# Half of the gate weights: the rounding remainder made by an adding transfer instead of a subtraction

## The chip, the cores and the metric

The kernel runs on one core of a Trainium2 chip. The core has an engine for matrix products (TensorE, in the profile PE, its weight loads PEld), three for elementwise work (VectorE or DVE, ScalarE or ACT, GpSimd or POOL), a queue that only issues transfers (SyncE or SP) and 16 DMA engines that carry out the transfers of all queues. Each engine works through its own instructions in a fixed order and waits on semaphores for the others. The metric is the device time of one execution in microseconds (us).

## What is computed

Two decoder layers over 512 tokens of width 2048: a Mamba-2 mixer in layer 0 and a stick-breaking attention in layer 1, each followed by a gated embedding. The change touches only the last, which stands in the reference once for each layer:

```python
for i in range(DEPTH):                       # DEPTH = 2
    u = rms_norm(h, norm_w[i])
    mix = ssd_branch(u, ...) if i % 2 == 0 else sb_branch(u, ...)
    h = h + mix
    gate = jax.nn.sigmoid((rms_norm(h, ple_norm_w[i]) @ ple_gate_w[i]))    # 2048 x 2048 weights
    h = h + (p[i] @ ple_proj_w[i]) * gate                                  # 256 x 2048 weights
```

## The kernel before

**Products.** Activations lie transposed, 128 channels on the partitions and 512 tokens along the free dimension, so a 2048-wide tensor is 16 tiles. A float32 product is made of three products in TensorE's faster, rounded 32-bit format (F32R). Weights and activations are split into a rounded part (`wh`, `ah`) and the remainder (`wl`, `al`), and `mm3` issues wh·ah, wh·al and wl·ah into one PSUM tile.

**Blocks.** Weights come in blocks of 8 tiles of 128 by 128 (512 KB, 128 partitions by 1024 numbers). `block` (L130 to L138) loads one from HBM over SP into `raw` (two buffers), ACT copies it into `wh` with rounding (three buffers), DVE subtracts, `wl = raw - wh` (three buffers), and TensorE uses it for 24 products of 512 columns.

**Gate stages.** `ple` (L513 on) runs once per layer. It splits the 16 tiles of `h` (`norm_acts`, L505), starts the norm's factor `rbc` from `ssq`, the sum of squares that POOL adds up (L503), and then makes 16 units of 128 output channels, j = 0 to 15, called u0 to u15 below. A unit is six products for p W in the PSUM tile `px_p` and a call of `unit` with two blocks, b0 and b1, 48 products in the PSUM tile `mm`. Behind them DVE multiplies by `rbc` (L532), ACT takes the sigmoid (L533), DVE multiplies by `px_p` (L534) and adds to `h` (L535). In layer 0 the square of the new `h` is then added to `ssq` (ACT L502, POOL L503), in layer 1 the tile of `h` goes out (L539). Every fourth unit also needs a block of `w_ple`, which keeps one of the three `wh` and `wl` buffers for four units; the other two pass between b0 and b1.

**Order.** TensorE's order is that of the program, by the class `Flow`. On the other engines a scheduler sets it when the kernel is built. `block` runs at high priority, so its steps stand as early as its buffers allow. The order is fixed on each engine, and an instruction that waits holds up all behind it.

Of the kernel before, what the change touches and what calls it, by code (L numbers as in the profile page):

```python
# [9 lines left out]
F32 = mybir.dt.float32  # L10
F32R = mybir.dt.float32r
AF = mybir.ActivationFunctionType
ALU = mybir.AluOpType
# [17 lines left out]
class Flow:  # L31
    """The tensor engine's instructions in the order in which they are traced.

    Side work is a generator that yields how many microseconds of products
    are to pass before it goes on, so that its operands are there by then."""

# [46 lines left out]
def trunk(  # L83
# [23 lines left out]

# [1 line left out]
    cst = cpool.tile([P, 4, P], F32, name="cst")  # L109
# [18 lines left out]

# [1 line left out]
    def block(src, offset=4000):  # L130
        with tc.high_priority(offset=offset):
            raw = wp.tile([P, 8, P], F32, tag="raw", name="raw", bufs=2)
            nc.sync.dma_start(raw, src)
            wh = wp.tile([P, 8, P], F32R, tag="wh", name="wh")
            S.copy(wh, raw)  # L135
            wl = wp.tile([P, 8, P], F32R, tag="wl", name="wl")
            V.tensor_tensor(wl, raw, wh.bitcast(F32), op=ALU.subtract)  # L137
        return wh, wl  # L138
# [15 lines left out]
    def staged(pool, tags, src, k0, k1):  # L154
        """Operands from tiles k0 to k1 of what was set down in DRAM."""
        acts = []
        for k in range(k0, k1):
            tag, bufs = tags[k % len(tags)]
            raw = pool.tile([P, T], F32, tag=tag, name="stg", bufs=bufs)
            nc.sync.dma_start(raw, src[k * P : (k + 1) * P, :])  # L160
            acts.append(act_tiles(k % KT))
            split(*acts[-1], raw)
        return acts
# [9 lines left out]

    def unit(src, acts):
        """One tile of 128 output channels: src is [128, nk, 128] in DRAM."""
        ps = mmp.tile([P, T], F32, tag="mm", name="mm")
        n = len(acts)
        for b in range(n // 8):
            wh, wl = block(src[:, 8 * b : 8 * b + 8, :])
            for k in range(8):  # L180
                kk = 8 * b + k
                mm3(ps, wh[:, k, :], wl[:, k, :], acts[kk][0], acts[kk][1], kk == 0, kk == n - 1)
                fl.poll()
        return ps

    def rsqrt(dst, ps, eps):
        """dst = (ps + eps) ** -0.5, with one Newton step behind the tables."""
        a = rp.tile([P, T], F32, tag="rsa", name="rsa")
        S.activation(a, ps, AF.Ln, bias=eps)
        S.activation(dst, a, AF.Exp, scale=-0.5)  # L190
        V.tensor_tensor(a, dst, dst, op=ALU.mult)
        V.scalar_tensor_tensor(a, ps, eps, a, op0=ALU.add, op1=ALU.mult)
        V.tensor_scalar(a, a, -0.5, 1.5, op0=ALU.mult, op1=ALU.add)
        V.tensor_tensor(dst, dst, a, op=ALU.mult)

    def act_set(name):
        """Loads a set of tables next after the ACT instructions so far."""
        with tc.high_priority(offset=100000):
            tc.keep_in_program_order(S.preload_act_table_set(name))

    def silu(dst, half, tmp):
        """x sigmoid(x) from x / 2: (tanh(x / 2) + 1) x / 2."""
        S.activation(tmp, half, AF.Tanh)  # L203
        S.activation(tmp, tmp, AF.Identity, bias=1.0)  # L204
        G.tensor_tensor(dst, half, tmp, op=ALU.mult)  # L205

    def row_scale(rbc, ssq, delay):
        """The norm's factor of each token, on every partition."""
        yield delay
        ps = px("px_n")  # L210
        fl.mm(ps, onesd, ssq)
        rsqrt(rbc, ps, eps6[:, 0:1])
# [5 lines left out]

    # ======== layer 0: SSD mixer ========
    with ExitStack() as st:  # L220
# [5 lines left out]
        acts = []  # L226
# [27 lines left out]

        # dt for the 64 heads and the first tile of B, side by side
        psd = mmp.tile([P, T], F32, tag="mm", name="psd")
# [17 lines left out]
        def dt_job():  # L274
            """dt = softplus(raw + bias), by token; the sums of a dt within chunks."""

# [7 lines left out]
            S.activation(e, e, AF.Exp, scale=-1.0)  # L284
            # log1p(e) = 2 atanh(e / (2 + e))
            V.tensor_scalar(z, e, 2.0, None, op0=ALU.add)
# [34 lines left out]

        # the convolution gives half of what silu takes
        V.tensor_scalar(vec[:, 128:368], vec[:, 128:368], 0.5, None, op0=ALU.mult)
# [18 lines left out]
        def scan(g, BT, CT, xc, zs):  # L342
            """The group's chunk scan, gate and norm."""
            hs = slice(g * HG, (g + 1) * HG)
            yield 11.0
            xdt, xw = [], []
            for c in range(NC):
# [18 lines left out]
                if c == 1:  # L366
                    # scores by source token, zero where the source comes later
                    pss = px("px_sc")
                    for c_ in range(NC):
                        cs = slice(c_ * P, (c_ + 1) * P)  # L370
                        fl.mm(pss[:, cs], BT[:, cs], CT[:, cs])
                    scT = sp.tile([P, NC, P], F32, tag="scT", name="scT")
                    V.tensor_tensor(
                        scT, pss.rearrange("p (c l) -> p c l", l=P), tri.unsqueeze(1).broadcast_to([P, NC, P]), op=ALU.mult
                    )
                    psb = px("px_bt")
                    for c_ in range(NC - 1):
                        fl.transpose(psb[:, c_ * P : (c_ + 1) * P], BT[:, c_ * P : (c_ + 1) * P], ident)
                    Bh = sp.tile([P, (NC - 1) * P], F32R, tag="Bh", name="Bh")
                    Bl = sp.tile([P, (NC - 1) * P], F32R, tag="Bl", name="Bl")  # L380
                    split(Bh, Bl, psb[:, : (NC - 1) * P])
                yield 4.0
                if c >= 1:
                    # states at the chunks' ends, [n, (h p)]
                    e = c - 1
# [96 lines left out]

        # the first units of the output projection, beside the last scan
        acts = staged(sp, [(f"xc{i}", 2) for i in range(4)], y_d, 0, KT)
# [7 lines left out]

    # ======== from here on the residual stays on chip ========
    lp = ctx.enter_context(tc.tile_pool(name="lp", bufs=1, reuse_waits="tile"))
# [18 lines left out]
    def ple(lq, layer, ssq):  # L513
        """h += (p W) sigmoid(norm(h) Wg), by tiles of 128 channels."""
        acts = norm_acts(plw[layer])
# [7 lines left out]
        for j in range(KT):  # L523
            if j % 4 == 0:
                vh, vl = block(w_ple[layer, j // 4])
            psp = px("px_p")
            for k in range(2):
                kk = 2 * (j % 4) + k
                mm3(psp, vh[:, kk, :], vl[:, kk, :], ph[:, k, :], pl[:, k, :], k == 0, k == 1)
            ps = unit(w_gate[layer, j], acts)  # L530
            gt = lq.tile([P, T], F32, tag="gt", name="gt", bufs=2)
            V.tensor_tensor(gt, ps, rbc, op=ALU.mult)  # L532
            S.activation(gt, gt, AF.Sigmoid)  # L533
            V.tensor_tensor(gt, psp, gt, op=ALU.mult)  # L534
            V.tensor_tensor(h[j], h[j], gt, op=ALU.add)  # L535
            if layer == 0:
                add_sq(lq, nssq, j)
            else:
                nc.sync.dma_start(out[j * P : (j + 1) * P, :], h[j])  # L539
# [17 lines left out]

    # ======== layer 1: stick-breaking attention ========
    with ExitStack() as st:
# [8 lines left out]
        def token_scale():  # L568
            """The factor of each token as one column to a chunk."""
            yield 20.0  # L570
# [7 lines left out]
        def values(m):  # L578
            """v of four heads by token, split."""
            pv = [mmp.tile([P, T], F32, tag="mm", name="pv") for _ in range(NC)]  # L580
# [42 lines left out]
        def attend(hd, done, vals):  # L623
# [9 lines left out]
            def scores(i):  # L633
# [5 lines left out]
                else:  # L639
                    mm3(pz, kh[:, ks], kl[:, ks], qh[:, qs], ql[:, qs])  # L640
                # log sigmoid(z) and -log sigmoid(-z)
                e = ap.tile([P, T], F32, tag="e", name="e", bufs=2)[:, :n]
# [12 lines left out]
                if i < NC - 1:  # L655
                    # with the same rows of the later blocks of sources
                    V.tensor_tensor(lm[:, P:], lm[:, P:], A[i + 1][2], op=ALU.add)
# [75 lines left out]

        # the first half of some output units, beside the last head
        half = staged(ap, [("stg", 3)], o_d, 0, 8)
# [19 lines left out]
def _units(w, cols):  # L755
    """[K, N] -> [units, 128 of K within a tile, K tiles, 128 columns]."""
    k = w.shape[0] // P
# [54 lines left out]
```

## Time and profile before

| | |
|---|---|
| two runs | 2759.84 and 2762.78 us, median 2761.31 us |
| span of the profiled execution | 2757.8 us |
| TensorE busy | 2732.7 us, 99% of the span |
| VectorE, ScalarE, GpSimd busy | 58%, 43%, 13% |
| HBM traffic | 108 GB/s on average |

The profiled execution has no time of its own beside its span, from the first to the last instruction. The span lies 3.5 us under the median of the runs, and what lies around it is not in the profile. Each gate stage takes some 200 us: the first from about 1373 to 1570 us, the second from about 2555 us to the end.

### The profile page before, as it was taken

Reading aid. Unit: us, or ns where it says so; the run is one execution under the profiler, and the core shown is the slowest. Engines: PE = TensorE matmul, PEld = TensorE weight load, DVE = VectorE, ACT = ScalarE, POOL = GpSimd, SP = SyncE. Lnnn points to the kernel's source line nnn. Section 1 sums busy time; section 2 is a strip of 40 time slices with the busy share of each in tenths; the row PEclk is TensorE's granted clock in tenths of the full one; section 3 lists DMA queues with packets and bytes.
Section 4 is the critical chain, followed back from the end, with each engine's and each line's share of the span. In section 5 each row is a group of like instructions: output and inputs, shape, how many; then the busy total and the mean of one; then the engine's idle time right before and its main releaser. Section 6 shows DMA issues by size and latency. Waiting matters only on the chain.

```text
span 2757.8 us, 32622 instructions
## 1 busy us (share of the span) xinstructions
PE 2732.7 (99%) x12684; PEld 2247.4 (81%) x12684; DVE 1597.3 (58%) x2226; ACT 1188.0 (43%) x1700; POOL 358.4 (13%) x363
## 2 busy tenths in 40 slices
PE   8999999999999999999999999999999999999999
PEld 6888888888888878888888888888888888888887
DVE  8676766676676774243443547647647647743533
ACT  5443444444353442232333436546646546533321
POOL 2222221212222120001101100000000000011000
PEclk9999999999999999999999999999999999999999
DMA  4342323233332446343323322322222222332332
GB/s 160 109 130 92 130 92 126 93 118 106 116 123 97 141 137 202 119 139 98 96 95 100 96 96 85 100 96 84 87 90 92 81 95 89 110 126 100 107 116 91
DMA packets 98348, 300.53 MB, mean 109 GB/s; under 512 B 10960, under 2 KB 11088, under 8 KB 98192
## 3 DMA queue, kind: packets, MB, share of 16 engines
q1 hardware_dynamic: 98192, 298.44, 33.2%
q8 instruction: 99, 1.62, 0.2%
q14 instruction: 57, 0.47, 0.1%
HBM read 280.18 MB, written 18.22 MB: 108 GB/s over the span
## 4 chain that ended last, share of the span: by engine, by line
PE 89%; DVE 5%; ACT 2%; POOL 2%; DMA 1%; issue 1%; SPq 0%; ACTq 0%; POOLq 0%; DVEq 0%
PE mm L54 74%; PE pv L54 6%; PE px_p L54 2%; DVE wl L137 1%; DVE M L410 1%; PE px_r L54 1%; PE px_z L54 1%; PE px_av L54 1%; POOL y L437 1%; PE px_st L54 1%; ACT wh L135 1%; PE px_y L54 1%; DMA stg<-y_d 1%; DVE cv L339 1%; PE px_qn L54 1%
## 5 line engine op out<-in xcount | busy, mean ns | idle before, releaser
L54 PE MATMUL mm<-ah,wh 128*128 128x512 f32 x3312 | 1300.1, 393 | 1.0 <-ACT ah L142 1.0
L54 PE MATMUL mm<-ah,wl 128*128 128x512 f32 x3312 | 1291.7, 390 | 0.0
L54 PE MATMUL mm<-al,wh 128*128 128x512 f32 x3312 | 1290.1, 390 | 1.5 <-DVE al L143 1.3
L137 DVE TENSOR_TENSOR wl<-raw,wh 128x1024 fp32r<-128x1024 f32 x457 | 569.9, 1247 | 492.3 <-ACT wh L135 491.2
L135 ACT CAST wh<-raw 128x1024 fp32r<-128x1024 f32 x457 | 478.7, 1048 | 856.7 <-PE mm L54 729.2
L54 PEld LDWEIGHTS mm<-ah,wl 128*128 128x128 f32 x3312 | 621.6, 188 | 131.9
L54 PEld LDWEIGHTS mm<-al,wh 128*128 128x128 f32 x3312 | 622.1, 188 | 130.9 <-DVE al L143 3.9
L54 PEld LDWEIGHTS mm<-ah,wh 128*128 128x128 f32 x3312 | 622.0, 188 | 126.3 <-ACT ah L142 1.2
L503 POOL TENSOR_TENSOR ssq<-ssq,sq 128x512 f32<-128x512 f32 x45 | 71.8, 1596 | 620.0 <-ACT sq L502 620.0
L410 DVE TENSOR_SCALAR M<-ab,act__370 128x128 f32<-128x128 f32 x256 | 104.8, 452 | 41.1 <-PE px_y L54 27.9
L339 DVE SCALAR_TENSOR_TENSOR cv<-xr,vec,cv 128x512 f32<-128x512 f32 x144 | 108.7, 755 | 7.0 <-ACT cv L337 4.4
L650 POOL TENSOR_SCALAR_AFFINE_SELECT lm<-lm 128x128 f32<-128x128 f32 x64 | 28.0, 438 | 615.3 <-DVE lm L649 609.6
L54 PE MATMUL pv<-wh,ah 128*128 128x512 f32 x256 | 101.0, 395 | 0.3 <-DVE gt L532 0.3
L54 PE MATMUL pv<-wl,ah 128*128 128x512 f32 x256 | 99.9, 390 | 0.0
L54 PE MATMUL pv<-wh,al 128*128 128x512 f32 x256 | 99.7, 389 | 0.0
L532 DVE TENSOR_TENSOR gt<-mm,rbc 128x512 f32<-128x512 f32 x32 | 22.1, 691 | 103.6 <-PE mm L54 103.6
L205 POOL TENSOR_TENSOR xc<-cv,sg 128x512 f32<-128x512 f32 x32 | 42.6, 1331 | 262.0 <-ACT sg L204 262.0
L203 ACT ACTIVATE sg<-cv 128x512 f32<-128x512 f32 x48 | 30.4, 633 | 104.6 <-DVE cv L339 104.3
L647 DVE SCALAR_TENSOR_TENSOR lb<-px_z,e 128x128 f32<-128x128 f32 (+1 forms) x64 | 31.4, 490 | 72.7 <-ACT e L645 72.2
L417 ACT ACTIVATE eA<-ab 64x384 f32<-64x384 f32 x64 | 33.6, 525 | 62.8 <-POOL y L437 60.3
L205 POOL TENSOR_TENSOR zs<-zs,sg 128x512 f32<-128x512 f32 x32 | 41.6, 1300 | 139.0 <-ACT sg L204 128.6
L337 ACT ACTIVATE cv<-xr,vec 128x512 f32<-128x512 f32 x48 | 39.0, 812 | 45.2 <-DVE xr L335 45.2
(219 smaller groups left out, 2557.9 us busy)
## 6 DMA issues: line engine op xcount, KB each, us to landing
raw<-in_w_in SPq DMA_DIRECT2D x160, 512.0 KB, 3.6
raw<-in_w_sb SPq DMA_DIRECT2D x96, 512.0 KB, 3.6
raw<-in_w_out SPq DMA_DIRECT2D x64, 512.0 KB, 3.9
raw<-in_w_gate SPq DMA_DIRECT2D x64, 512.0 KB, 3.5
ab<-ac_d SPq DMA_DIRECT2D x64, 256.0 KB, 3.2
raw<-in_w_v SPq DMA_DIRECT2D x32, 512.0 KB, 3.6
raw<-in_w_sbo SPq DMA_DIRECT2D x32, 512.0 KB, 3.5
y_d<-zs SPq DMA_DIRECT2D x32, 256.0 KB, 4.3
```

The costliest lines, as they stand in the source:

```text
L54: self._queue(self.tc.nc.tensor.matmul(out, lhsT, rhs, start=start, stop=stop), rows / 2370.0)
L135: S.copy(wh, raw)
L137: V.tensor_tensor(wl, raw, wh.bitcast(F32), op=ALU.subtract)
L203: S.activation(tmp, half, AF.Tanh)
L205: G.tensor_tensor(dst, half, tmp, op=ALU.mult)
L337: S.activation(cv, xr[:, 3 : T + 3], AF.Identity, bias=cb[:, u : u + 1], scale=cw[:, u, 3:4])
L339: V.scalar_tensor_tensor(cv, xr[:, tap : tap + T], cw[:, u, tap : tap + 1], cv, op0=ALU.mult, op1=ALU.add)
L410: V.tensor_scalar(M[:, c, :], ab[:, c * P : (c + 1) * P], act_[:, c, h : h + 1], act_[:, c, h : h + 1], op0=ALU.min, op1=ALU.subtract,)
L417: S.activation(eA[pp, :], ab[pp, P:], AF.Exp)
L503: G.tensor_tensor(ssq, ssq, sq, op=ALU.add)
L647: V.scalar_tensor_tensor(lb, pz, 0.0, e, op0=ALU.min, op1=ALU.subtract)
L650: G.affine_select(out=lm[:, :P], in_=lm[:, :P], compare_op=ALU.is_gt, fill=0.0, base=0, pattern=[[1, P]], channel_multiplier=-1,)
```

## The change

In the 16 units of each gate stage, b1 (`b % 2 == 1`) no longer gets its remainder from DVE. ACT writes the negated copy, `wl = -wh`, and a transfer from SBUF to SBUF on POOL's queue adds `raw` to it, `wl += raw`. b0, the blocks of `w_ple` and all other weights stay as they were. It concerns 32 of 457 blocks. Lines of the changed kernel lie seven further down from here on; comments and docstrings were taken out, which changes nothing.

```diff
-    def block(src, offset=4000):
+    def block(src, offset=4000, add=False):
         with tc.high_priority(offset=offset):
             raw = wp.tile([P, 8, P], F32, tag="raw", name="raw", bufs=2)
             nc.sync.dma_start(raw, src)
             wh = wp.tile([P, 8, P], F32R, tag="wh", name="wh")
             S.copy(wh, raw)
             wl = wp.tile([P, 8, P], F32R, tag="wl", name="wl")
-            V.tensor_tensor(wl, raw, wh.bitcast(F32), op=ALU.subtract)
+            if add:
+                S.mul(wl, wh.bitcast(F32), -1.0)
+                G.dma_start(wl, raw, accum_op=ALU.add)
+            else:
+                V.tensor_tensor(wl, raw, wh.bitcast(F32), op=ALU.subtract)
         return wh, wl
...
-    def unit(src, acts):
+    def unit(src, acts, add=False):
         ps = mmp.tile([P, T], F32, tag="mm", name="mm")
         n = len(acts)
         for b in range(n // 8):
-            wh, wl = block(src[:, 8 * b : 8 * b + 8, :])
+            wh, wl = block(src[:, 8 * b : 8 * b + 8, :], add=add and b % 2 == 1)
...
-            ps = unit(w_gate[layer, j], acts)
+            ps = unit(w_gate[layer, j], acts, add=True)
```

ACT in the second gate stage, units 0 to 2, before. The `gt` rows are the sigmoids of u0, u1 and u2; the two `wh` rows ahead of each are b0 and b1 of the next unit.

```order
L533 ACT_TABLE_LOAD
L533 ACTIVATE gt_19805<-gt_19805 128x512
L135 CAST wh_19895<-raw_19893 128x1024
L135 CAST wh_19925<-raw_19923 128x1024
L533 ACTIVATE gt_19879<-gt_19879 128x512
L135 CAST wh_19969<-raw_19967 128x1024
L135 CAST wh_19999<-raw_19997 128x1024
L533 ACTIVATE gt_19953<-gt_19953 128x512
```

The same place after the change.

```order
L540 ACT_TABLE_LOAD
L540 ACTIVATE gt_19822<-gt_19822 128x512
L141 ACTIVATE wl_19870<-wh_19868 128x1024
L138 CAST wh_19913<-raw_19911 128x1024
L138 CAST wh_19943<-raw_19941 128x1024
L540 ACTIVATE gt_19897<-gt_19897 128x512
L141 ACTIVATE wl_19945<-wh_19943 128x1024
L138 CAST wh_19988<-raw_19986 128x1024
L138 CAST wh_20018<-raw_20016 128x1024
L540 ACTIVATE gt_19972<-gt_19972 128x512
L141 ACTIVATE wl_20020<-wh_20018 128x1024
```

The negated copy of b1 of unit j+1 stands behind the sigmoid of unit j, not right behind its own rounding copy.

POOL at the start of the first gate stage, after the change. Before, the adds into `ssq` stand alone; `wl_10553` is b1 of u0, `wl_10628` of u1 and so on; `ssq_8607` is the sum that this stage's norm needs, and the add shown is its last.

```order
L142 DMA wl_10553<-raw_10549 128x1024
L510 TENSOR_TENSOR ssq_8607<-ssq_8607,sq2_10421 128x512
L142 DMA wl_10628<-raw_10624 128x1024
L142 DMA wl_10705<-raw_10701 128x1024
L510 TENSOR_TENSOR ssq_10495<-ssq_10495,sq2_10660 128x512
L142 DMA wl_10782<-raw_10778 128x1024
L510 TENSOR_TENSOR ssq_10495<-ssq_10495,sq2_10737 128x512
```

The adding transfer of b1 of u0 now stands ahead of the last add of the sum; later the transfer of u(j+1) stands ahead of the add of unit j.

## Rows read from the trace of the kernel before

**Rows 1.** The page: span, busy time of each engine, granted TensorE clock by slice.

```profile
span 2757.8 us, 32622 instructions
PE 2732.7 (99%) x12684; PEld 2247.4 (81%) x12684; DVE 1597.3 (58%) x2226; ACT 1188.0 (43%) x1700; POOL 358.4 (13%) x363
PEclk9999999999999999999999999999999999999999
```

**Rows 2.** Busy time by stretch, inside the two gate stages (window, length, busy by engine).

```profile
1386.00:1496.00 110.00, 110.00 (x487) 91.08 (x486) 42.09 (x47) 32.67 (x39) 10.26 (x8) 1.00 0.30 100
2568.00:2752.00 184.00, 183.88 (x812) 151.93 (x810) 68.58 (x78) 42.73 (x48) 0.00 (x0) 1.00 0.32 108
```

**Rows 3.** Chain that ended last, second gate stage: start, length, engine and tile.

```profile
2629.49 1.36 PE px_p L54 x6
2630.84 10.88 PE mm L54 x48
2641.72 1.36 PE px_p L54 x6
```

**Rows 4.** Timeline of TensorE and its weight loads, one unit of that stage.

```profile
2629.10 0.39 PE L54 MATMUL mm<-ah,wl 128*128 128x512 f32 x1
2629.32 0.39 PE L54 MATMUL px_p<-ph,wh 128*128 128x512 f32 x1
...
2636.35 0.19 PEld L54 LDWEIGHTS mm<-ah,wl 128*128 128x128 f32 x1
```

**Rows 5.** Timeline of ACT, the same unit.

```profile
2629.30 1.05 ACT L135 CAST wh<-raw 128x1024 fp32r<-128x1024 f32 x1 [4.34 <-PE mm L54]
2630.26 0.62 ACT L533 ACTIVATE gt<-gt 128x512 f32<-128x512 f32 x1
2636.14 1.05 ACT L135 CAST wh<-raw 128x1024 fp32r<-128x1024 f32 x1 [5.26 <-issue]
```

**Rows 6.** Timeline of DVE, the same unit.

```profile
2629.52 0.69 DVE L532 TENSOR_TENSOR gt<-mm,rbc 128x512 f32<-128x512 f32 x1 [3.31 <-PE mm L54]
2630.38 1.23 DVE L137 TENSOR_TENSOR wl<-raw,wh 128x1024 fp32r<-128x1024 f32 x1 [0.17 <-ACT wh L135]
2631.52 0.68 DVE L534 TENSOR_TENSOR gt<-px_p,gt 128x512 f32<-128x512 f32 x1
```

**Rows 7.** Groups of the page: rounding copy, and POOL's add.

```profile
L135 ACT CAST wh<-raw 128x1024 fp32r<-128x1024 f32 x457 | 478.7, 1048 | 856.7 <-PE mm L54 729.2
L503 POOL TENSOR_TENSOR ssq<-ssq,sq 128x512 f32<-128x512 f32 x45 | 71.8, 1596 | 620.0 <-ACT sq L502 620.0
```

**Rows 8.** DMA view of 2570 to 2750 us: packets, MB, share of 16 engines; issues.

```profile
q1 hardware_dynamic: 6480, 19.66, 32.5%
...
raw<-in_w_gate SPq DMA_DIRECT2D x27, 512.0 KB, 3.5
out<-h SPq DMA_DIRECT2D x15, 256.0 KB, 2.7
```

**Rows 9.** Timeline of ACT, POOL and TensorE, start of the first gate stage.

```profile
1373.10 1.04 ACT L135 CAST wh<-raw 128x1024 fp32r<-128x1024 f32 x1
1374.05 0.72 ACT L145 ACTIVATE ah<-h,vec 128x512 fp32r<-128x512 f32 x1
1375.22 0.63 ACT L502 ACTIVATE sq<-h 128x512 f32<-128x512 f32 x1 [0.46 <-DVE h L554]
...
1387.13 1.28 ACT L533 ACT_TABLE_LOAD   x1
...
1376.00 2.07 POOL L503 TENSOR_TENSOR ssq<-ssq,sq 128x512 f32<-128x512 f32 x1 [9.79 <-ACT sq L502]
...
1378.38 1.02 PE L54 MATMUL px_n<-ssq,onesd 128*128 128x512 f32 x2
...
1380.86 0.19 PEld L54 LDWEIGHTS mm<-ah,wl 128*128 128x128 f32 x1
```

## The prediction

> **What bounds the kernel now.** The page is read first: TensorE is busy 2732.7 of 2757.8 us, at the full granted clock in every slice [rows 1]. So only what makes TensorE wait can cost time, and only what ends a wait of TensorE can gain any. The windows inside the two gate stages say the same more sharply: 110.00 of 110.00 us and 183.88 of 184.00 us are busy, while DVE has 42 and 69 us of work there and ACT 33 and 43 [rows 2]. The work that the change takes from DVE ended no wait. The question is whether the new way of making `wl` stays ahead of TensorE.
>
> The chain that ended last gives TensorE's rhythm: six products for `px_p` in 1.36 us and 48 for `mm` in 10.88 us, 12.24 us a unit, 0.227 us a product [rows 3]. The timelines of the same unit then tell how far ahead the weights are. Unit j ends at 2629.32, when `px_p` of unit j+1 begins. At 2629.30 ACT makes `wh` of b1 of unit j+1; it was waiting for TensorE, that is, for the buffer that b1 of unit j had just given up [rows 4, 5]. DVE's subtraction runs from 2630.38 to 2631.61 [rows 6]. TensorE loads the first tile of this `wl` at 2636.35: 1.36 us of `px_p`, 5.44 us of b0 and two products of b1 after the unit's start [rows 4]. The subtraction has 4.7 us to spare, no more: although the pool has three buffers, b1 is prepared only one block ahead.
>
> **The change part by part.** It removes 32 subtractions of 1.23 us from DVE [rows 6]. Nothing waits for them, so this is worth nothing on the path; the steps behind them (`px_p` times the gate at 2631.52, the add to `h`) come some 0.5 us earlier, which only the end of a stage could use, and no b1 is left to be made there.
>
> It adds 32 copies on ACT. A copy of this shape takes 1.05 us [rows 7], and ACT has about 8 us free in a unit. What matters is its place: in the order shown with the change, it stands behind the sigmoid of unit j. The sigmoid can't start before unit j has ended and DVE has multiplied (2629.52 to 2630.21); it ran from 2630.26 to 2630.88 [rows 5, 6]. ACT's instructions overlap by about 0.1 us there (the copy from 2629.30 lasts to 2630.35, the sigmoid starts at 2630.26), so the negated copy ends at about 2631.85. From there to the weight load at 2636.35 there is a **window of 4.5 us** for everything that is left: POOL's turn, the transfer and the semaphore to TensorE.
>
> It adds 32 transfers on POOL. Call X the time from the end of the negated copy to the moment when TensorE may load `wl`. If X is over 4.5 us, TensorE stops at the third product of b1, the unit ends later by X - 4.5, and the next unit's sigmoid, copy and transfer start later by as much. The delay isn't made up by running ahead, since every negated copy hangs on the end of the unit before. So a unit takes 12.24 + max(0, X - 4.5) us.
>
> X isn't in this trace, as no transfer adds and none is issued by POOL. I put it together from three pieces. The first is a plain transfer of the same size: the gate weights' loads land 3.5 us after their issue [rows 8]. The second is the read of the destination, which an adding transfer must make as well as that of its source. In 2570 to 2750 us 19.66 MB took 32.5% of 180 us, which is 336 GB/s while the engines move, or 1.56 us for 512 KB [rows 8]; so 1.6 us more if the second read costs what the first does. The Trainium skill, "Collectives: The Full Stack", section "The bandwidth ceiling: the fold count and why AG ≠ RS ≠ AR", says that a transfer that adds is slower not for the addition but because it needs two source reads, and gives it about half the rate; no transfer of this trace shows that, and without it X would be 1.6 us shorter. The third piece is POOL's part, taking up the semaphore and preparing the transfer in software. Its bounds are nothing, and the longest pass over a tile that rows 9 show, 2.07 us; the usual pass takes 1.6 [rows 7, 9]. I take 1.3, nearer to the pass since 128 rows have to be described for two sources and one destination. X = 3.5 + 1.6 + 1.3 = **6.4 us**. The ends are 3.6 (a second read that is hidden, 0.1 us on POOL) and 9.1 (two landings of 3.5 one behind the other and 2.1 on POOL).
>
> With 6.4 a unit waits 1.9 us. This holds for u1 to u15 of both stages: 30 x 1.9 = 57 us. The first units differ. In u1 a load of activation tables (1.28 us) [rows 9] lies between the copy and the sigmoid, so the window is 1.3 us shorter: 2 x 1.3 = 2.6 us. In u0 the negated copy stands behind the split of `h` tile 14 and ahead of the square of tile 15. It would run from about 1374.7 to 1375.7, push the square back by 0.5 us, and on POOL the transfer's 1.3 us would come ahead of the last add into `ssq`. That add ended at 1378.07, and the product that needs it ran at 1378.38, so only 0.3 us were spare [rows 9]: about 0.8 us later. The remainder of u0's b1 is needed at 1380.86 [rows 9], by then 1381.7, which leaves it 6.0 us against 6.4: 0.4 us. Together 1.3 in each stage, 2.6 us. The **sum is 57 + 2.6 + 2.6 = 62 us**, on a span of 2757.8: 2820 us. The runs shown lie about 3.5 us above the span at their median, so the forecast is 2761 + 62 = 2823 us.
>
> Three other waits come with the change and cost nothing by this count. The load of the next b1 into `raw` waits for the transfer in place of DVE. From the end of the transfer it takes 3.5 us, then follow copy, sigmoid and negated copy (2.6 us) and X: a cycle of X + 6.1 against the period of X + 7.7, so 1.6 us are spare at any X. On SP the stores of `h` stand behind such a load only where the transfer has ended before the store is due. On POOL the add of unit j stands behind the transfer for u(j+1), which was due earlier; the store of 256 KB (2.7 us) [rows 8] goes out while the transfer runs in the second stage, and may take some tenths of it.
>
> **The rivals.** First, **the transfer fits into the window**: SBUF answers faster than HBM, POOL needs little, and X is at most 4.5. What speaks for it is that the 3.5 us [rows 8] contain a read from HBM. Against it speaks that a second read and POOL's part together may take only 1.0 us. The decision falls at X = 4.5. At 4.4, u1 would still wait 1.2 us and u0 0.8, twice: 4 us, 2765 us, not slower. The Trainium skill, "DMA: Bandwidth & Descriptors", section "Anatomy of one DMA — SWDGE (gpsimd) path", gives a transfer issued by GpSimd 2.0 us plus its bytes at 436 GB/s. For the two reads, 1.05 MB, my estimate from that is 4.4 us, this rival's case; the same figures give a plain load of 512 KB 3.2 us, where this trace has 3.5, on another queue. I give it 0.2.
>
> Second, **the addition itself is slow**, more than one pass of extra movement for each byte. Nothing in the trace speaks for or against it, since nothing in it adds in flight. With three passes more than a load (3 x 1.6) and POOL at 1.7, X is 10.0, and the wait 5.5 us: 30 x 5.5 = 165 us, with 2 x 5 for the first units 2936 us. Chance 0.19.
>
> Third, **the `raw` buffer becomes the bound**: with the traffic of the transfers, loads land later than the 5.1 us that the cycle above leaves them. At 7 us, two landings in a row, 1.9 us a unit come on top of my forecast, 2880 us. HBM and SBUF traffic together stay under half of the engines' time (32.5% before, and at most twice 1.56 us more in 12.24), so 0.05.
>
> A gain would need a wait of TensorE that the change ends, and the gate stages have none [rows 2]: 0.01. That the change doesn't do what it says is excluded by the order, which has the copies and transfers in place of the subtractions.
>
> **How the numbers follow.** My forecast, X between 4.5 and 8.3, has 0.55; it reaches from 2765 to 2883 us. A measurement of this kernel can tell about 2%, 55 us, from no change. That is reached at X = 6.2, just under my value, so the forecast's own case is split: 0.23 under and 0.32 over. Within 2%: 0.23 + 0.2 = 0.43. Slower: 0.32 + 0.19 + 0.05 = 0.56. Faster: 0.01. The range begins at 2760, where the first rival ends, takes in the end of X = 9.1 (2909 us) and stops at 2925, with about half of the second rival left out.
>
> **What would show it.** In the profile after, TensorE should wait for the transfer of `wl` 30 times, about 1.9 us each, always at the third product of b1; the negated copy should start within 0.1 us of the sigmoid's end; and a unit should take 14.1 us in both stages, 12.24 everywhere else. The landing time of the transfers on POOL's queue gives X directly, and each microsecond by which it misses moves the sum by 32. The forecast is wrong if the negated copy runs ahead of the sigmoid, if the transfer takes under 4.5 or over 8.3 us, or if the granted clock falls in the gate stages once TensorE has gaps; no row before has such gaps at a lower clock.

## Result, and the profile after

The changed kernel takes 2786.1 us at the median of two runs (2785.89 and 2786.31), before 2761.3 us. The ratio is 1.0089, with a 95% interval of 1.0059 to 1.0118: 25 us slower, where 62 were forecast. That is clear of the noise, inside the stated range, and under the 2% that the forecast took as the step to slower.

First the page of the changed kernel, in the lines that answer to [rows 1] and [rows 7], with the groups that are new or have changed most (behind the bar: busy time, mean of one, idle time before and its releaser).

```profile
span 2784.6 us, 32699 instructions
PE 2744.0 (99%) x12684; PEld 2246.1 (81%) x12684; DVE 1560.4 (56%) x2194; ACT 1218.1 (44%) x1732; POOL 388.2 (14%) x395
...
L54 PE MATMUL mm<-ah,wl 128*128 128x512 f32 x3312 | 1295.8, 391 | 15.1 <-DMA wl<-raw 15.0
...
L54 PEld LDWEIGHTS mm<-ah,wl 128*128 128x128 f32 x3312 | 622.0, 188 | 158.6 <-DMA wl<-raw 27.7
...
L142 POOL DMA_DIRECT2D wl<-raw x32 | 27.9, 871 | 362.5 <-ACT wl L141 342.9
```

The span grew by 26.8 us. TensorE's weight loads now wait 27.7 us for the adding transfer, and before they waited for nothing here. The view of their waits has the count (engine and tile, what was waited for: us in total, times, longest).

```profile
PEld mm L54 <- DMA wl<-raw: 27.7, 30, 2.7
```

These are the thirty waits of the forecast, one for each unit but the first of a stage, of 0.9 us instead of 1.9 at the mean.

The chain that ended last, for a unit of the first gate stage, beside [rows 3]:

```profile
1438.91 1.36 PE px_p L54 x6
1440.27 5.89 PE mm L54 x26
1446.17 0.01 issue
1446.18 5.28 PE mm L54 x22
1451.46 1.36 PE px_p L54 x6
```

The 48 products come in two pieces now, 26 and 22: TensorE stops at the third product of b1. The unit takes 12.55 us, 0.3 more than before. In the second stage the same chain reads as follows.

```profile
2594.01 1.05 ACT wl L141
2595.07 0.29 issue
2595.36 4.92 DMA wl<-raw
2600.28 0.04 issue
2600.32 5.07 PE mm L54 x21
2605.39 0.03 ACTq L138
2605.42 0.04 issue
2605.46 0.95 ACT wh L138
```

Here a turn of the chain is all links: negated copy, 0.29 us to POOL's issue, 4.92 us to the landing, TensorE's last products, and the next unit's rounding copy. The unit takes 12.93 us. The timelines of ACT and POOL in the first stage answer to [rows 5].

```profile
1451.32 1.06 ACT L138 CAST wh<-raw 128x1024 fp32r<-128x1024 f32 x1 [4.74 <-PE mm L54]
1452.27 0.62 ACT L540 ACTIVATE gt<-gt 128x512 f32<-128x512 f32 x1
1452.80 1.05 ACT L141 ACTIVATE wl<-wh 128x1024 fp32r<-128x1024 f32 x1
...
1454.15 0.87 POOL L142 DMA_DIRECT2D wl<-raw  x1 [10.19 <-ACT wl L141]
```

The negated copy ends at 1453.85, 2.53 us after the rounding copy's start, and 2.55 were worked out. So the window was right, and X is what differs. The DMA views of the two stages, 1400 to 1570 and 2590 to 2770 us, give it (last column: issue to landing, median; one fence for each).

```profile
raw<-in_w_gate SPq DMA_DIRECT2D x25, 512.0 KB, 3.8
wl<-raw POOLq DMA_DIRECT2D x14, 512.0 KB, 4.5
```

```profile
raw<-in_w_gate SPq DMA_DIRECT2D x25, 512.0 KB, 3.9
wl<-raw POOLq DMA_DIRECT2D x14, 512.0 KB, 5.0
out<-h SPq DMA_DIRECT2D x14, 256.0 KB, 2.0
```

X is 0.29 + 4.5 + 0.04 = 4.8 us in the first stage and 5.3 in the second. Over a window of 4.5 that makes waits of 0.3 and 0.8; the ordinary units are longer by 0.3 and by 0.7 to 0.8.

Where the 26.8 us lie, by the starts of `px_p` in TensorE's timeline (before, every unit from u1 on takes 12.24 us):

| | first stage | second stage |
|---|---|---|
| u0 (13.14 before) | 13.83 | 13.82 |
| u1 | 13.98 | 16.01 |
| ordinary units of u2 to u14 | 12.50 to 12.58 | 12.93 to 13.04 |
| longer ones of u2 to u14 | u3, u7, u11, u12: 12.84 to 12.93 | u3, u7, u11: 13.66 to 13.72; u4: 14.84 |
| over before, u0 to u14 | 7.7 us | 18.0 us |

The remaining 1.1 us lie behind the start of the second stage's last unit. In u1 of the second stage 1.7 us are TensorE's clock (last section).

### The profile page after: what moved, and what is told of

Its sections match the earlier page's. It is cut to its first block, busy times and chain, and to the rows that moved or that the text cites. A ratio compares the mean times of both kernels' runs of the same rounds, so it can differ in the third digit from the quotient of the medians.

```text
span 2784.6 us, 32699 instructions
## 1 busy us (share of the span) xinstructions
PE 2744.0 (99%) x12684; PEld 2246.1 (81%) x12684; DVE 1560.4 (56%) x2194; ACT 1218.1 (44%) x1732; POOL 388.2 (14%) x395
## 4 chain that ended last, share of the span: by engine, by line
PE 82%; DVE 6%; DMA 5%; ACT 4%; issue 2%; POOL 2%; SPq 0%; ACTq 0%; POOLq 0%; DVEq 0%
PE mm L54 68%; PE pv L54 6%; DMA wl<-raw 4%; ACT wh L138 1%; DVE wl L144 1%; DVE M L417 1%; PE px_r L54 1%; PE px_z L54 1%; PE px_av L54 1%; POOL y L444 1%; DVE al L153 1%; ACT wl L141 1%; PE px_st L54 1%; DMA stg<-y_d 1%; PE px_y L54 1%
## 5 line engine op out<-in xcount | busy, mean ns | idle before, releaser
L144 DVE TENSOR_TENSOR wl<-raw,wh 128x1024 fp32r<-128x1024 f32 x425 | 530.2, 1248 | 514.9 <-ACT wh L138 514.0
L54 PEld LDWEIGHTS mm<-ah,wl 128*128 128x128 f32 x3312 | 622.0, 188 | 158.6 <-DMA wl<-raw 27.7
L142 POOL DMA_DIRECT2D wl<-raw x32 | 27.9, 871 | 362.5 <-ACT wl L141 342.9
```

What stands on the lines that cost most here:

```text
L54: self._queue(self.tc.nc.tensor.matmul(out, lhsT, rhs, start=start, stop=stop), rows / 2370.0)
L142: G.dma_start(wl, raw, accum_op=ALU.add)
```

## The experiments

All of them change the changed kernel in a few lines; the loss is given against the kernel before, measured with it (2760.6 to 2760.9 us).

**The place of the negated copy.** ACT makes it from `raw` and not from the rounded copy, which gives the same number.

```diff
-                S.mul(wl, wh.bitcast(F32), -1.0)
+                S.mul(wl, raw, -1.0)
```

> The negated copy is made from raw instead of from the rounded copy, so it stands right behind the rounding copy and ahead of the sigmoid of the unit before. Theory (the window is set by the negated copy's place, X is 4.9 us in the first gate stage and 5.3 in the second): the window grows from 4.5 to 5.0 us, the first stage waits no more (12.24 us a unit), the second 0.2 to 0.3 us a unit, and the second unit of each stage loses its extra wait: about 2768 us. Rival (TensorE waits for the transfer because of traffic on the DMA engines, not because of when it starts): units stay at 12.5 and 13.0 us, about 2785 us.

Measured: 2763.8 us, ratio 1.0009 (1.0000 to 1.0019). ACT's timeline shows the new order:

```profile
2634.31 1.06 ACT L138 CAST wh<-raw 128x1024 fp32r<-128x1024 f32 x1 [4.39 <-PE mm L54]
2635.27 1.05 ACT L141 ACTIVATE wl<-raw 128x1024 fp32r<-128x1024 f32 x1
2636.23 0.62 ACT L540 ACTIVATE gt<-gt 128x512 f32<-128x512 f32 x1
```

The copy starts 0.96 us after the rounding copy instead of 1.48, and with as many transfers as before nine tenths of the loss are gone. Ordinary units take 12.24 us in both stages. By the starts of `px_p` the two stages lose 1.8 us together, against 25.7 in the changed kernel, and 1.1 of it is in u4 of the second stage. The rival, traffic, is out as the main cause.

Part of what is left in this profile lies ahead of the first gate stage. TensorE's granted clock (third column from the end) was 0.50 in this stretch, and 1.00 in the same stretch of the changed kernel's profile:

```profile
1036.10:1042.90 6.80, 5.95 (x27) 5.04 (x28) 2.79 (x5) 0.00 (x0) 1.01 (x1) 0.50 0.45 149
```

The profiles of seven other variants below have 3.4 us at half the clock at about this place. So where a total is a few microseconds over the kernel before, the units tell better than the total what the change costs.

**Buffers of its own for b1.**

```diff
-            raw = wp.tile([P, 8, P], F32, tag="raw", name="raw", bufs=2)
+            raw = (own or wp).tile([P, 8, P], F32, tag="raw", name="raw", bufs=2)
...
-            wh = wp.tile([P, 8, P], F32R, tag="wh", name="wh")
+            wh = (own or wp).tile([P, 8, P], F32R, tag="wh", name="wh", bufs=2 if own else 3)
...
-            wl = wp.tile([P, 8, P], F32R, tag="wl", name="wl")
+            wl = (own or wp).tile([P, 8, P], F32R, tag="wl", name="wl", bufs=2 if own else 3)
...
-            wh, wl = block(src[:, 8 * b : 8 * b + 8, :], add=add and b % 2 == 1)
+            wh, wl = block(src[:, 8 * b : 8 * b + 8, :], add=add and b % 2 == 1, own=own if b % 2 == 1 else None)
...
-            ps = unit(w_gate[layer, j], acts, add=True)
+            ps = unit(w_gate[layer, j], acts, add=True, own=lq)
```

> The blocks with the adding transfer get two raw, wh and wl buffers of their own. Theory (b1 is prepared only one block ahead, and a wait of 0.3 to 0.7 us is what X has over that): with a whole unit ahead nothing waits but the first unit of each stage, 12.24 us a unit, about 2763 us. Rival (the transfers cost TensorE time as traffic, or the sum comes from elsewhere): the time stays over 2775 us.

Measured: 2775.6 us, ratio 1.0050 (1.0035 to 1.0065), so by the total the rival had it, and by the stages the theory. Busy time by stretch inside the two gate stages (window, length, TensorE busy, and so on):

```profile
1390.00:1560.00 170.00, 170.00 (x752) 140.81 (x751) 49.66 (x60) 60.76 (x73) 28.89 (x27) 1.00 0.52 133
2585.00:2755.00 170.00, 170.00 (x752) 140.77 (x751) 48.44 (x59) 50.88 (x57) 12.05 (x14) 1.00 0.54 146
```

TensorE waits for nothing there; every unit from u1 on takes 12.24 us, and u0 13.15 as before. The loss came about outside, in the output projection of the attention. With buffers free early, the first gate blocks moved forward, into the loads of that stage: their loads start at 2410.9 us and two adding transfers at 2418.2 and 2421.4, which land after 9.4 and 9.6 us. The waits of TensorE there, 2420 to 2575 us, and the longest piece of the chain ahead of them:

```profile
PE mm L54 <- ACT ah L149: 9.3, 2, 8.2
```

```profile
2418.29 11.19 DMA pr<-in_pT
```

TensorE waited 8.2 us at a stretch for activations that ACT could not split, behind a copy that waited for a load landing after 11.2 us. Within that wait TensorE's clock fell to half, and it stayed there for 13.6 us:

```profile
2430.40:2444.00 13.60, 7.26 (x15) 4.70 (x16) 5.85 (x8) 4.65 (x8) 0.00 (x0) 0.50 0.58 196
```

TensorE was busy for 7.3 us of them, which at the full clock would have been about 3.6 us less. This estimate and the 9.3 us of waits are nearly all of the 13.2 us by which the second gate stage starts later after the first than it does in the kernel before.

**The other block of the unit.**

```diff
-            wh, wl = block(src[:, 8 * b : 8 * b + 8, :], add=add and b % 2 == 1)
+            wh, wl = block(src[:, 8 * b : 8 * b + 8, :], add=add and b % 2 == 0)
```

> The first block of each unit gets the adding transfer in place of the second: as many copies and transfers, another place. Its negated copy hangs on no sigmoid, and from its end there are about 5.0 us until TensorE needs it. Theory (place): no wait in the first stage, 0 to 0.3 us a unit in the second, about 2765 us. Rival (cost by the transfer itself, wherever it stands): about 2786 us as in the changed kernel.

Measured: 2770.2 us, ratio 1.0033 (1.0020 to 1.0046). Two thirds of the loss are gone though the work is the same. 21 of the 30 unit lengths from u0 to u14 lie within 0.05 us of 12.24; what is left stands in the first units and mostly around the blocks of `w_ple`, 0.4 to 1.3 us each. That is more than the theory had, and on its side.

**What the second read costs.** The transfer copies instead of adding.

```diff
-                G.dma_start(wl, raw, accum_op=ALU.add)
+                G.dma_start(wl, raw)
```

> The transfer copies and doesn't add, so wl becomes raw and the gates are computed with a wrong remainder; the negated copy and all else stay. It measures what the second read costs. Theory (a second read as dear as the first, 1.3 to 1.6 us): the landing falls from 4.5 (first stage) and 4.9 us to about 3.2 and 3.5, no unit waits, about 2763 us. Rival (the second read is hidden): the landing stays at 4.5 and 4.9, about 2785 us.

Measured: 2765.1 us, ratio 1.0012 (1.0003 to 1.0022). Ordinary units take 12.24 us in both stages. The DMA view of this run, POOL's queue (packets, MB, share of 16 engines) and its transfers:

```profile
q0 software_dynamic: 4608, 16.78, 1.6%
...
wl<-raw POOLq DMA_DIRECT2D x32, 512.0 KB, 3.0
```

In the changed kernel the same queue has:

```profile
q0 software_dynamic: 4608, 16.78, 3.3%
...
wl<-raw POOLq DMA_DIRECT2D x32, 512.0 KB, 4.9
```

The engines are busy twice as long for the same bytes: 3.3% of 2784.6 us over 32 transfers is 2.9 us each, 1.6% of 2763.6 is 1.4. These landings are medians of both stages, with the stores of the second in them. In the first stage alone, 1400 to 1570 us, the plain transfer has:

```profile
wl<-raw POOLq DMA_DIRECT2D x14, 512.0 KB, 2.9
```

The adding one took 4.5 there, so the second read costs 1.6 us of landing. Some 0.3 us of this are POOL's issue, 0.87 us against 0.53 to 0.57.

**The same plain transfer, issued by SP.**

```diff
-                G.dma_start(wl, raw, accum_op=ALU.add)
+                nc.sync.dma_start(wl.bitcast(F32), raw)
```

> As the run in which the transfer copies and doesn't add, but issued by SP, whose loads from HBM land 3.5 us after their issue; the gates are computed with a wrong remainder. It measures what of these 3.5 us is HBM. Theory (the source in SBUF answers sooner, and my 3.5 us counted a way from HBM that this transfer hasn't): it lands after about 2.5 us. Rival (3.5 us belong to SP's kind of issue and to the size): about 3.5 us.

Measured once: 2761.2 us, no wait in the first stage. From its DMA view:

```profile
raw<-in_w_gate SPq DMA_DIRECT2D x64, 512.0 KB, 3.6
...
wl<-raw SPq DMA_DIRECT2D x32, 512.0 KB, 2.9
```

On the same queue, at the same size, a source in SBUF lands 0.7 us sooner than one in HBM. Issued by POOL it lands at most 0.1 us later than by SP (2.9 us each in the first stage).

**The stores of the second stage.** All but the last are left out.

```diff
-                nc.sync.dma_start(out[j * P : (j + 1) * P, :], h[j])
+                if j == KT - 1:
+                    nc.sync.dma_start(out[j * P : (j + 1) * P, :], h[j])
```

> In the second gate stage only the last of the 16 tiles of h is stored, so 15/16 of the output stays unwritten. Theory (the store, issued 0.2 us after the transfer, is what makes its landing 4.9 us there and 4.5 in the first stage): the landing falls to 4.5, a unit of the second stage to 12.5 us as in the first, 0.4 us x 15 = 6 us less, about 2779 us. Rival (the second stage is slower for another reason): landing and units stay at 4.9 and 13.0, 2785 us.

Measured: 2778.1 us, ratio 1.0062 (1.0047 to 1.0077), 8 us less than the changed kernel. Its second stage, 2590 to 2770 us, has the first stage's landing, and ordinary units of 12.50 to 12.60 us:

```profile
wl<-raw POOLq DMA_DIRECT2D x14, 512.0 KB, 4.5
```

So the store, issued 0.2 us behind the transfer, costs it 0.4 us at the median. Without the stores u0 to u14 of the second stage lose 7.8 us, as in the first stage; u1 takes 13.95 us instead of 16.01.

**Raw buffers of its own.** As the second experiment, for `raw` alone.

```diff
-            raw = wp.tile([P, 8, P], F32, tag="raw", name="raw", bufs=2)
+            raw = (own or wp).tile([P, 8, P], F32, tag="raw", name="raw", bufs=2)
```

> The blocks with the adding transfer get two raw buffers of their own, wh and wl stay as they were. Theory (the long units, 13.7 and 14.8 us around a block of w_ple in the second stage, come from loads that were held until the transfer had ended, bunch up and meet the next transfer): those units fall to 13.0, some 4 us less, about 2781 us. Rival (raw buffers bound nothing): the same units stay long, 2785 us.

Measured: 2787.6 us, ratio 1.0097 (1.0080 to 1.0114), nothing gained. The units around a block of `w_ple` stay at 13.66 to 14.02 us; only u4 is shorter, by 0.8. That theory falls: these units are not long because `raw` is held. In the changed kernel a load of the next block is issued at 2610.21, in the middle of the transfer from 2608.29 to 2613.94, which lands after 5.65 us. It is the same in u7 and u11: a load comes 1.9 us behind the transfer, which lands after 5.7 us, and in the ordinary units without such a load after 4.9 to 5.0. In the first stage the transfers with such a load (u3, u7, u11, u15) land after 4.8 to 4.9 us and all others after at most 4.7. That the load and the transfer disturb each other fits this, but it was only read from the traces.

**No transfer at all.**

```diff
                 S.mul(wl, wh.bitcast(F32), -1.0)
-                G.dma_start(wl, raw, accum_op=ALU.add)
```

> The adding transfer is left out, so wl is the negated rounded copy and the gates are computed wrongly; DVE's subtraction stays away and ACT's second copy stays. Theory (neither the freed DVE nor the added ACT work moves the end, all of the loss is the transfer): 12.24 us a unit, 2761 us. Rival (ACT's copy costs something by its place, or DVE's freedom gains something): more than 2 us away from 2761.

Measured: 2761.3 us, ratio 1.0002 (0.9993 to 1.0011), every unit from u1 on at 12.24 us. The subtraction's absence gains nothing. ACT's copy costs nothing there, and 0.7 us in u0 of each stage: u0 takes 13.83 and 13.84 us instead of 13.14, with no transfer in the kernel. The product for the norm's factor waits 0.4 us for the last add into `ssq` there, whose square stands behind the copy.

**The chain made longer.**

```diff
+                S.mul(wl, wh.bitcast(F32), -1.0)
                 S.mul(wl, wh.bitcast(F32), -1.0)
```

> The negated copy is written twice, one after the other, which puts 0.95 us more into the chain ahead of each transfer. Theory (each unit is the chain from the end of the unit before, sigmoid, copy, transfer, and TensorE's last 22 products, so what is added comes out in full): 0.95 us x 30 units = 29 us over the changed kernel, about 2814 us, units of 13.5 and 13.9 us. Rival (the waits are chance collisions of transfers): under 10 us more.

Measured: 2849.0 us, ratio 1.0318 (1.0303 to 1.0334), 63 us over the changed kernel where 29 were expected. Ordinary units take 13.60 to 13.71 us in both stages, 1.07 over the first stage's 12.55: the second copy waits for the end of the first, so it adds 1.05 and not 0.95. In the second stage the transfer is now issued after the store, and its wait is no longer than in the first. So what is added does come out in full. The other half is in six units of 18.3 to 19.7 us, the ones where a block of `w_ple` is prepared. Their chain shows why:

```profile
2708.54 0.93 ACT wh L138
2709.47 0.97 ACT wl L142
2710.44 0.29 issue
2710.73 6.94 DMA wl<-raw
2717.67 0.04 issue
2717.71 7.30 PE mm L54 x21
```

The rounding copy of the `w_ple` block stands between the two negated copies, the transfer lands after 6.9 us beside a load issued at 2710.76, and then 21 products take 7.30 us instead of 5.07, part of them at half the clock (last section).

**Two halves.**

```diff
-                G.dma_start(wl, raw, accum_op=ALU.add)
+                G.dma_start(wl[:, :4, :], raw[:, :4, :], accum_op=ALU.add)
+                G.dma_start(wl[:, 4:, :], raw[:, 4:, :], accum_op=ALU.add)
```

> The adding transfer is split into two, tiles 0 to 3 and tiles 4 to 7 of the block, issued one after the other. TensorE needs the second half 12 products, 2.7 us, after the first. Theory (a transfer's landing is 0.9 us of issue, about 1.3 us fixed and 2.9 us that grow with its size): the first half lands at about 3.2 us after its issue, the second by 5.2, both inside their windows, so the waits go: about 2766 us. Rival (issue and fixed part dominate): each half lands after 4 us or more, the second 5 us or more, no gain, about 2785 us or more.

Measured: 2771.5 us, ratio 1.0037 (1.0022 to 1.0052). From u2 on three units in four take 12.24 to 12.3 us in the first stage; the units around `w_ple`, and u1, keep 12.6 to 13.3 us. The first half has a shorter X, so the waits go where no other transfer comes in, and the estimate was 5 us too good where one does.

**Both remedies.** The negated copy from `raw`, and two halves.

> Both remedies together: the negated copy made from raw, ahead of the sigmoid, and the transfer in two halves. Theory (the loss is the window alone): nothing is left to wait for in steady units, 2762 us, not under the kernel before, whose TensorE never waited here. Rival (DVE's freed time or the shorter DVE chain gives something once the waits are gone): under 2757 us.

Measured: 2762.6 us, ratio 1.0004 (0.9995 to 1.0014). All units of the first stage from u1 on take 12.24 us. It can't be told from the kernel before, and isn't faster: no version of the change gained anything.

## Why the prediction was wrong

**What bounds the kernel** was right. Taking the subtraction away gained nothing, and ACT's added copy alone cost 0.7 us in u0 of each stage and nothing elsewhere (no transfer at all: 2761.3 us).

**The window** was right. The negated copy stood behind the sigmoid and ended where it was worked out, TensorE stopped at the third product of b1, thirty times, and whatever lengthened the chain came out in each unit (0.3 us over in the first stage, 0.7 to 0.8 in the second, 1.07 more with a second copy). Moving the copy ahead of the sigmoid by 0.5 us took nine tenths of the loss away, and buffers that let b1 run ahead took it out of the gate stages.

**X was mis-sized**: 6.4 us foretold, 4.8 and 5.3 measured. This is the step that failed, "X = 3.5 + 1.6 + 1.3". Its pieces by the runs:

- The second read, 1.6: it costs 1.6 us of landing, 0.3 of them in the issue, and 1.5 us of the engines' time. Right. The Trainium skill, "Collectives: The Full Stack", section "The bandwidth ceiling: the fold count and why AG ≠ RS ≠ AR", gives a reduction between cores about half the rate of a copy for its two source reads. The traces agree for this transfer within one core: 3.3% against 1.6% of the engines' time.
- The plain transfer, 3.5: this was the landing of a load from HBM. From SBUF it is 2.9 us on the same queue. Too long by 0.6.
- POOL's part, 1.3: 0.29 us from the end of the copy to the issue, and at most 0.1 us by which POOL's plain transfer lands later than SP's. Its issue of 0.87 us is part of the landing, which counts from the issue's start; I had added POOL's preparation on top. Too long by 1.0.

Together 1.6 us too much, 0.29 + 2.9 + 1.6 = 4.8. As the window takes 4.5 of it, an X that was a third too long made the wait six times too long in the first stage: 1.9 us instead of 0.3.

The Trainium skill, "DMA: Bandwidth & Descriptors", section "Anatomy of one DMA — SWDGE (gpsimd) path", gives by its figures 4.4 us for both reads and 3.2 for one, the estimate behind the first rival. The traces are near it, 4.5 and 2.9 us of landing in the first stage.

I had given that rival 0.2. What it left out is the 0.29 us ahead of the issue, which put X just past the window instead of just inside. X did fall into the forecast's own case, 4.5 to 8.3, but near its lower end, and the outcome was the one within 2%, which had 0.43, and not slower, which had 0.56.

**Smaller terms.** The first unit was foretold 1.3 us longer and is 0.7: the late add into `ssq` was foretold at 0.8 and comes even without a transfer, and the 0.4 for the remainder didn't occur, as X stayed under 6.0. The second unit's extra, 1.3 for the load of tables, is 1.4 in the first stage (1.74 less 0.3). The store's share, "some tenths", is 0.4 us a unit; I had named it and left it out of the sum, and without the stores the second stage costs no more than the first. The third rival, `raw` as the bound, had the wrong mechanism: buffers of its own gained nothing. The traffic beside it was also summed wrongly: 32.5% and twice 1.56 us in 12.24 make 58% of the engines' time and not "under half", and the changed kernel shows 50% in the first stage (1390 to 1560 us) and 53% in the second (2595 to 2765).

What stays open is why u4 of the second stage takes 14.84 us. Its transfer landed after 6.8 us, and the one at that place was late in most variants too (5.1 to 6.0 us in six of them). The DMA view of 2620 to 2628.5 us has a packet of another queue there:

```profile
q8 instruction: 1, 0.02, 1.4%
```

Such a packet falls into the transfer of this unit in each of these six runs too, and in the changed kernel no other transfer meets one while its bytes move. That it holds the transfer up fits, but no run tried it.

## What to carry to other kernels

When work is moved to a transfer, write down the window between the earliest start and the first use, and the chain that closes it; if that chain starts at the end of the loop's own last product, every tenth of a microsecond over the window is paid in every turn. A duration taken from another kind of transfer has parts that the new one lacks, and an issue that the landing time already counts must not be added to it; where window and estimate are a microsecond apart, the uncertainty of the sum can be larger than the forecast loss. A step that needs only the input, not the rounded copy, can be placed earlier for nothing, and deeper buffers can move loads into a stage where they hurt.

## What the runs showed of the hardware

During or after some waits TensorE's clock fell to half. In the second unit of the second stage TensorE had waited 1.83 us for the transfer, and then the window has:

```profile
2585.70:2592.50 6.80, 6.75 (x22) 5.37 (x23) 0.00 (x0) 0.00 (x0) 0.00 (x0) 0.75 0.50 157
```

The granted clock is 0.75 in the mean of these 6.8 us (third column from the end): the last 22 products took 6.8 us instead of 5.0, and seven of them followed each other at 0.43 us instead of 0.23, at 1.2 GHz, half of the full 2.4. With the copy made twice it came in the long units, around waits of over 4 us:

```profile
2711.00:2717.00 6.00, 2.40 (x11) 1.67 (x9) 0.72 (x1) 1.04 (x1) 0.59 (x1) 0.89 0.80 175
2717.00:2720.00 3.00, 2.29 (x5) 1.83 (x6) 0.51 (x1) 0.00 (x0) 0.00 (x0) 0.50 0.44 102
```

A wait of 2.31 us in u4 of the second stage was followed by the full clock. So was one of 3.0 us for DVE, which ends at about 1036 us, in the kernel before and in the changed one, while at the end of the same wait the run with the copy from `raw` has the half clock shown there. So the length of the wait alone doesn't decide. The forecast had named the clock as a risk and given it no price; here it cost 1.7 us. In the run with two copies the mean granted clock is 0.96 from 1370 to 1600 us and 0.95 from 2600 to 2790, so at most some 19 us of its loss are the clock's.
